# Left operands of the first w_up group: made at the start of the up stage, or in the dense stage and kept in DRAM

## The chip, the cores and the metric

The kernel runs on one core of one Trainium2 chip. The metric is the device time of one execution in microseconds, so lower is better. The core has TensorE (PE) for matmuls, VectorE (DVE), ScalarE (ACT), GpSimd (POOL) and SyncE (SP). DMAs are issued from the queues of SP, ACT and POOL.

## The reference

One layer of an encoder on 2048 tokens of width 1024, all in fp32:

```python
h = rms_norm(x, norm_mix[l])
z = h @ w_in[l]                      # 1024 -> q, k, v of two attentions and two gates
...
merged = (gates[..., :D_MODEL] * (y_a @ w_proj_a[l])
          + gates[..., D_MODEL:] * (y_b @ w_proj_b[l]))
x = x + merged @ w_out[l]
h2 = rms_norm(x, norm_mlp[l])
x = x + jnp.square(jax.nn.relu(h2 @ w_up[l])) @ w_down[l]    # 1024 -> 4096 -> 1024
return rms_norm(x, norm_final)
```

y_a is attention within a window of 128 tokens, y_b attention within a neighbourhood of a token grid.

## The kernel before

Every fp32 operand of a matmul is split into a rounded part (hi, a cast on ScalarE, L277) and the rest (lo, a subtraction, L278), and a product is the sum of three fp32r matmuls, hi·hi, hi·lo and lo·hi (L281, L282, L283). The large products are done by blocks of 2 x 2 with Strassen's seven products, so both operands are also sums and differences of blocks; a product is named by its number n from 1 to 7.

The stages follow each other in time: the dense stage (w_in, up to about 540 us), the two attentions and gates (to about 1170), the out stage (w_out, two halves m of the tokens, to about 1370), the up stage (w_up, to about 1993) and the down stage (w_down).

*Dense stage.* Quads q = 2 to 13 of columns of w_in are computed one after the other (`in_seeded`); each quad has seven products, and beside each product one step of a generator `prep` is issued. Such generators prepare later stages: `wo_parts` makes the left operands of the out stage from w_out and keeps them in DRAM (wo_d), `h1_sums` makes sums of right pages (h1sum). Their small tiles zc (ring `in_c`) and xin are shared with the stage's own work. The tiles of v (quads 6 and 12) are turned by TensorE (L392, from zc into PSUM), cast by ScalarE (L405), subtracted by VectorE (L406) into ze and written by SP to vs_b (L456).

*Up stage.* Its left operands are parts of w_up: for each group q of 512 columns `up_left_steps` makes seven operands [128, 2, 4, 256] (hi and lo, 1 MB) from two raw tiles uraw, in rings uwhla (one buffer) and uwhlb (two). Its right operands are pages ubh of h2, read back from DRAM (h2d) into uraw and urb, scaled (L548 on ScalarE, L551 on VectorE) or cast and subtracted. The order of the products is 1, 5, 6, 2, 7, 4, 3. An output block is emptied from PSUM (tile b) into uc. The first group's work is issued within the out stage's second half, m = 1, by `up_start`: `up_weights` loads two raw tiles (L1265), products 1 and 5 have their lo parts on VectorE, and the steps from product 6 on use GpSimd (`eng=G`): its rows are L272 (differences) and L278 (lo parts).

The program is written in issue order, and a scheduler that goes by the modelled times of the whole program sets the order on each engine's queue. So a change in one place shifts instructions near it and near those that depend on it. Within a queue the order is kept: what stands behind a waiting instruction waits too. A name such as zv stands for a tile that may belong to a ring of one or more buffers; a new user of a buffer waits until the last reader has finished.

Of the kernel before, what the change touches and what calls it, by code (L numbers as in the profile page):

```python
# [8 lines left out]
F32 = mybir.dt.float32  # L9
F32R = mybir.dt.float32r  # L10
AF = mybir.ActivationFunctionType
ALU = mybir.AluOpType
# [10 lines left out]
P = 128  # L23
KC = D // P
NB = 4
BT = 512
# [66 lines left out]
def encoder_layer(ctx, tc, x, norm_mix, w_in, b_gate, sink, rpb, w_pa, w_pb, w_out,  # L93
                  norm_mlp, w_up, w_down, norm_final, dist_a, mask_b, out):
    nc = tc.nc
    V, A, G, PE, SY = nc.vector, nc.scalar, nc.gpsimd, nc.tensor, nc.sync
# [16 lines left out]
    dp = pool("dp", space=DRAM)  # L113
# [157 lines left out]
    def add(eng, out, a, b, op=ALU.add):  # L271
        return eng.tensor_tensor(out=out, in0=a, in1=b, op=op).ins  # L272
# [400 lines left out]
    def wo_parts(k, own):  # L673
# [24 lines left out]
        for n, src in ((2, b21), (5, t1), (7, t3), (6, b12), (4, b11)):  # L698
            part(n, src)
            yield  # L700

    def own():
        return T(xp, [P, D], F32, "xin", 3)

# [52 lines left out]
    for q in range(2, len(QUADS)):  # L757
        if q != SECOND + 1:
            prep = iter(())
        steps, b0 = 1, 0  # L760
        if q == 5:
            prep = wo_parts(0, own)
        elif q in (6, 7):
            k = 2 * (q - 6)
            prep, steps = in_turn((h1_sums(k), h1_sums(k + 1))), 2
        elif q == SECOND - 1:
            prep = h1_right(right2)
        elif q == len(QUADS) - 1:
            prep = h1_last(right2)
        elif q >= SECOND and q != SECOND + 1:  # L770
            n_wo[0] += 1
            prep = wo_parts(n_wo[0], own)
        if q == SECOND:
            right, b0 = right2, 2
        elif q > SECOND:
            b0 = 2
        next(prep, None)
        if q == 11:
            bias_tables()
        lf = list(in_left(ws, QUADS[q][1], (1, 2) if q == 2 else (), ORDER if q == 2 else ORDER_3))  # L780
# [475 lines left out]
    def up_whl():  # L1256
        n_whl[0] += 1
        return (up_rings["whla"] if n_whl[0] % 3 == 1 else up_rings["whlb"])()

    def up_weights(q, behind=None):  # L1260
        ws = []
        for p in range(2):
            w = up_rings["raw"]()
            with tc.issue_after(behind) if behind else nullcontext():
                SY.dma_start(w, w_up[0][p * BT : (p + 1) * BT, q * BT : (q + 1) * BT].rearrange("(k p) f -> p k f", p=P))  # L1265
            ws.append(w)
        return ws
# [5 lines left out]
            pass  # L1273
        return out

    def up_left_steps(ws, out, behind=None, eng=V):

        a11, a21 = ws[0][:, :, 0:256], ws[0][:, :, 256:512]
        a12, a22 = ws[1][:, :, 0:256], ws[1][:, :, 256:512]

        def parts(src, eng):
            hl = up_whl()
            split(src, hl[:, 0], hl[:, 1], eng)
            return hl
# [9 lines left out]
        add(eng, a21, a11, a21, ALU.subtract)  # L1294
        s2 = up_rings["S"]()
        add(eng, s2, a22, a21, ALU.subtract)
        out[6] = parts(s2, eng)
        yield
        out[2] = parts(a12, eng)
        yield  # L1300
        out[7] = parts(a21, eng)
        yield
        out[4] = parts(a22, eng)
        last_left[0] = rounded[0]
        yield
        add(eng, a12, a12, s2, ALU.subtract)
        out[3] = parts(a12, eng)
# [201 lines left out]
    def up_start():  # L1509

        up_homes("raw", "whla", "whlb", "bh1", "bh5", "S")
        rights, lf = up_right(0), {}
        next(rights)
        yield
        next(rights)
        ws = up_weights(0, wo_dma[0])
        yield
        rest = up_left_steps(ws, lf, eng=G)
        started.extend((rights, lf, rest))
        for _ in range(2):  # L1520
            next(rest)
        yield
# [169 lines left out]
    for m in range(2):  # L1692
# [4 lines left out]
        ws = None  # L1697
# [200 lines left out]
```

## Time and profile before

| What | Value |
|---|---|
| Times of three runs | 2610.56, 2615.22, 2616.41 us; median 2615.22 |
| Profiled execution | 2613.9 us, span 2612.1 us, mean granted clock 0.996 |
| Busy in the span: PE, DVE, ACT, POOL | 97%, 65%, 50%, 16% |
| DMA | 552.39 MB, mean 211 GB/s |

In the rows of the profile, a time at the left is the start in the span, the next number the duration; a group's row gives its count behind an x, then the busy time and the mean of one. In square brackets stands how long the engine had been idle and what released it. A row of waits gives the total, how often, and the longest. A window's row gives for PE, PEld (weight load), DVE, ACT and POOL the busy microseconds and the number of instructions, then the granted clock of TensorE, the share of DMA time that was busy, and GB/s. DMA rows give the issue's line and queue (SPq, ACTq, POOLq), the size, and the time from issue to landing.

### The profile page before, as it was taken

Reading aid. Unit: us, or ns where it says so; the run is one execution under the profiler, and the core shown is the slowest. Engines: PE = TensorE matmul, PEld = TensorE weight load, DVE = VectorE, ACT = ScalarE, POOL = GpSimd, SP = SyncE. Lnnn points to the kernel's source line nnn. Section 1 sums busy time; section 2 is a strip of 40 time slices with the busy share of each in tenths; the row PEclk is TensorE's granted clock in tenths of the full one; section 3 lists DMA queues with packets and bytes.
Section 4 is the critical chain, followed back from the end, with each engine's and each line's share of the span. In section 5 each row is a group of like instructions: output and inputs, shape, how many; then the busy total and the mean of one; then the engine's idle time right before and its main releaser. Section 6 shows DMA issues by size and latency. Waiting matters only on the chain.

```text
span 2612.1 us, 34574 instructions
## 1 busy us (share of the span) xinstructions
PE 2546.5 (97%) x11936; PEld 2116.3 (81%) x11936; DVE 1702.0 (65%) x2693; ACT 1310.8 (50%) x2345; POOL 412.2 (16%) x506
## 2 busy tenths in 40 slices
PE   7999999999999998999998999999999999999998
PEld 6788888877877987888887888888887888888887
DVE  8867577667675575745589667766665535554766
ACT  6365464557765674614356555644444322323444
POOL 1000101133345764221312000000000000000011
PEclk9999999999999999999999999999999999999999
DMA  5768868774348998788887665854428825445554
GB/s 186 217 197 247 282 226 275 234 219 114 93 137 208 223 273 233 228 283 315 271 330 246 234 226 201 290 169 152 155 103 303 299 97 185 145 151 164 185 197 166
DMA packets 347695, 552.39 MB, mean 211 GB/s; under 512 B 32072, under 2 KB 152376, under 8 KB 345472
## 3 DMA queue, kind: packets, MB, share of 16 engines
q1 hardware_dynamic: 330336, 509.66, 61.0%
q10 hardware_dynamic: 10944, 24.12, 2.5%
q0 software_dynamic: 6240, 16.40, 2.1%
q8 instruction: 94, 1.54, 0.2%
q14 instruction: 81, 0.66, 0.1%
HBM read 363.35 MB, written 186.71 MB: 211 GB/s over the span
## 4 chain that ended last, share of the span: by engine, by line
PE 76%; DMA 11%; DVE 7%; ACT 3%; issue 2%; SPq 1%; POOL 1%; DVEq 0%; POOLq 0%; ACTq 0%
PE b L282 15%; PE b L283 15%; PE b L281 15%; PE zb L281 5%; PE zb L283 5%; PE zb L282 5%; PE mm L202 2%; PE mm L204 2%; PE mm L203 2%; DMA vb<-vs_b 2%; PE av L1117 1%; DMA z<-zg 1%; PE pt L1137 1%; PE pt L887 1%; DMA uraw<-h2d 1%
## 5 line engine op out<-in xcount | busy, mean ns | idle before, releaser
L282 PE MATMUL b<-dwh,dah 128*128 128x512 f32 x896 | 348.7, 389 | 0.4 <-DVE dwh L278 0.4
L283 PE MATMUL b<-dwh,dah 128*128 128x512 f32 x896 | 347.7, 389 | 0.0
L281 PE MATMUL b<-dwh,dah 128*128 128x512 f32 x896 | 338.3, 389 | 1.6 <-ACT dwh L277 1.6
L277 ACT CAST dah<-da 128x1024 fp32r<-128x1024 f32 (+1 forms) x128 | 120.9, 945 | 368.6 <-PE b L283 245.8
L281 PE MATMUL zb<-zh,zwhl 128*128 128x512 f32 x728 | 284.3, 391 | 4.8 <-DVE zc L272 2.0
L282 PE MATMUL zb<-zh,zwhl 128*128 128x512 f32 x728 | 284.7, 391 | 0.0
L283 PE MATMUL zb<-zh,zwhl 128*128 128x512 f32 x728 | 283.4, 391 | 1.2 <-DVE zwhl L278 1.1
L278 DVE TENSOR_TENSOR dah<-da,dah 128x1024 fp32r<-128x1024 f32 (+1 forms) x128 | 139.2, 1089 | 213.9 <-ACT dah L277 212.0
L281 PE MATMUL b<-ubh,uwhlb 128*128 128x512 f32 x592 | 230.2, 389 | 2.6 <-ACT uc L1472 1.6
L282 PE MATMUL b<-ubh,uwhlb 128*128 128x512 f32 x592 | 230.4, 389 | 1.2 <-DVE ubh L278 1.2
L283 PE MATMUL b<-ubh,uwhlb 128*128 128x512 f32 x592 | 229.0, 389 | 0.0
L281 PEld LDWEIGHTS b<-dwh,dah 128*128 128x128 f32 x896 | 168.2, 188 | 36.9 <-ACT dwh L277 2.1
L282 PEld LDWEIGHTS b<-dwh,dah 128*128 128x128 f32 x896 | 168.2, 188 | 35.7 <-DVE dwh L278 0.8
L283 PEld LDWEIGHTS b<-dwh,dah 128*128 128x128 f32 x896 | 168.2, 188 | 34.8
L272 DVE TENSOR_TENSOR uc<-b,uc 128x512 f32<-128x512 f32 x160 | 109.1, 689 | 114.2 <-PE b L283 107.8
L281 PEld LDWEIGHTS zb<-zh,zwhl 128*128 128x128 f32 x728 | 136.7, 188 | 35.3 <-ACT zc L488 2.5
L283 PEld LDWEIGHTS zb<-zh,zwhl 128*128 128x128 f32 x728 | 136.7, 188 | 30.4 <-DVE zwhl L278 2.5
L282 PEld LDWEIGHTS zb<-zh,zwhl 128*128 128x128 f32 x728 | 136.7, 188 | 27.7
L202 PE MATMUL mm<-zh,whl 128*128 128x512 f32 x368 | 155.7, 423 | 0.6 <-ACT z L465 0.6
L204 PE MATMUL mm<-zh,whl 128*128 128x512 f32 x368 | 145.5, 395 | 0.0
L203 PE MATMUL mm<-zh,whl 128*128 128x512 f32 x368 | 145.0, 394 | 0.0
L281 PEld LDWEIGHTS b<-ubh,uwhlb 128*128 128x128 f32 x592 | 111.1, 188 | 26.3 <-ACT uc L1472 2.0
(268 smaller groups left out, 5734.9 us busy)
## 6 DMA issues: line engine op xcount, KB each, us to landing
at<-uc SPq DMA_DIRECT2D x224, 256.0 KB, 2.9
da<-at SPq DMA_DIRECT2D x96, 512.0 KB, 3.5
dw<-in_w_down_dram SPq DMA_DIRECT2D x160, 256.0 KB, 5.0
uraw<-in_w_up_dram SPq DMA_DIRECT2D x32, 1024.0 KB, 5.9
pgl<-wo_d SPq DMA_DIRECT2D x28, 1024.0 KB, 7.2
zraw<-in_w_in_dram SPq DMA_DIRECT2D x24, 1024.0 KB
z<-zg SPq DMA_DIRECT2D x64, 256.0 KB, 4.7
qs_a<-ze SPq DMA_DIRECT2D x32, 256.0 KB, 5.4
```

The source lines that it names most:

```text
L202: PE.matmul(ps, lh, rh, start=first, stop=False)
L203: PE.matmul(ps, lh, rl, start=False, stop=False)
L204: PE.matmul(ps, ll, rh, start=False, stop=last)
L272: return eng.tensor_tensor(out=out, in0=a, in1=b, op=op).ins
L277: rounded[0] = A.copy(hi, src).ins
L278: return eng.tensor_tensor(out=lo, in0=src, in1=hi.bitcast(F32), op=ALU.subtract).ins
L281: PE.matmul(ps, lh, rh, start=first, stop=False, skip_group_check=True)
L282: PE.matmul(ps, lh, rl, start=False, stop=False, skip_group_check=True)
L283: PE.matmul(ps, ll, rh, start=False, stop=last, skip_group_check=True)
L887: last = PE.transpose(pt[:, h * P : (h + 1) * P], s[:, h, c * P : (c + 1) * P], ident).ins
L1117: PE.matmul(po[0][:, i0 * P : (i0 + ni) * P], v[:kp, c, :], src[:kp, o : o + ni * P], start=first[0], stop=(c == 7 and z == 1), skip_group ...
L1137: last = PE.transpose(pt[:kp, at + (i - i0) * P : at + (i - i0 + 1) * P], s[i][:, rr : rr + kp], ident)
```

## The change

A new tile `wu_d` in DRAM holds the seven left operands of the first group of w_up. A new generator `wu_parts(k)` makes one of four quarters of them in each of the dense quads 6, 7, 9 and 12: two loads of 256 KB on SP into the tile zv (one buffer), sums and differences on VectorE, four casts on ScalarE, four subtractions on VectorE, and four writes each from ScalarE's and GpSimd's queues. At the start of the up stage `up_loaded` reads the seven operands from `wu_d` by GpSimd's queue. The raw loads, casts, sums and subtractions of the first group's left operands are gone there, and `up_left_steps` has no GpSimd work any more; for the other groups it stays as it was.

```diff
+    WU = (1, 7, 2, 4, 5, 6, 3)
+    wu_d = dp.tile([len(WU), P, 2, 4, 256], F32, name="wu_d")
+
+    def wu_parts(k):
+
+        t = in_v2()
+        for p in range(2):
+            SY.dma_start(t[:, p * BT : (p + 1) * BT], w_up[0][(4 * p + k) * P : (4 * p + k + 1) * P, 0:BT])
+        yield
+        a11, a21, a12, a22 = (t[:, j * 256 : (j + 1) * 256] for j in range(4))
+        u = [in_c(), in_c()[:, 0:256]]
+        s1, s2 = (u[0][:, j * 256 : (j + 1) * 256] for j in range(2))
+        add(V, s1, a21, a22)
+        add(V, a21, a11, a21, ALU.subtract)
+        yield
+        add(V, s2, a22, a21, ALU.subtract)
+        add(V, u[1], a12, s2, ALU.subtract)
+        for n, src in zip((4, 6, 0, 2), (*u, t[:, 0:BT], t[:, BT : 2 * BT])):
+            yield
+            w = src.ap[-1][1]
+            hi = in_c()[:, 0:w]
+            A.copy(hi.bitcast(F32R), src)
+            V.tensor_tensor(out=src.bitcast(F32R), in0=src, in1=hi, op=ALU.subtract)
+            dst = wu_d[n : n + w // 256].rearrange("n p z k c -> p n z k c")
+            for z, part, queue in ((0, hi, A), (1, src, G)):
+                queue.dma_start(dst[:, :, z, k], part.rearrange("p (n c) -> p n c", c=256))
...
+        prep_up = wu_parts((6, 7, 9, 12).index(q)) if q in (6, 7, 9, 12) else iter(())
         next(prep, None)
+        next(prep_up, None)
...
+            next(prep_up, None)
...
+    def up_loaded(out):
+
+        for n in (1, 5, 6, 2, 7, 4, 3):
+            out[n] = up_whl()
+            G.dma_start(out[n].bitcast(F32), wu_d[WU.index(n)])
+            yield
...
-    def up_left_steps(ws, out, behind=None, eng=V):
+    def up_left_steps(ws, out, behind=None):
...
         next(rights)
-        ws = up_weights(0, wo_dma[0])
-        yield
-        rest = up_left_steps(ws, lf, eng=G)
+        yield
+        rest = up_loaded(lf)
```

The change moves instructions on each engine. First SP in the dense stage, where the v tiles of quad 6 are written (vs_b), before:

```order
L456 DMA vs_b_92<-ze_2268 128x1x512 x2
L710 DMA xin_2461<-h1d_96 128x512
L456 DMA vs_b_93<-ze_2292 128x1x512 x2
L710 DMA xin_2461<-h1d_97 128x512
L710 DMA xin_2625<-h1d_96 128x512
L456 DMA vs_b_94<-ze_2323 128x1x512 x2
L710 DMA xin_2625<-h1d_97 128x512
L456 DMA vs_b_95<-ze_2346 128x1x512 x2
```

The same place after; L709 is the load of w_up rows for quad 7's `wu_parts`, and L737 is what was L710:

```order
L456 DMA vs_b_93<-ze_2307 128x1x512 x2
L737 DMA xin_2491<-h1d_96 128x512
L737 DMA xin_2491<-h1d_97 128x512
L456 DMA vs_b_94<-ze_2343 128x1x512 x2
L709 DMA zv_272_2496<-in_w_up_dram 128x512 x2
L456 DMA vs_b_95<-ze_2366 128x1x512 x2
L737 DMA xin_2669<-h1d_96 128x512
L737 DMA xin_2669<-h1d_97 128x512
```

The new load stands ahead of the writes of five of the eight tiles of v, and it waits for the last write from the same buffer by GpSimd's queue.

Second ScalarE at the start of the up stage, from the scaling of page 2 (L548) on, before. ubh_1611 is the hi part of page 7, ubh_1613 that of page 4, and L1434 copies product 2 out of PSUM:

```order
L548 ACTIVATE ubh_1598_13559<-urb_13557,g_mix 128x512 x4
L277 CAST uwhlb_13578<-uraw_13185 128x1024
L277 CAST uwhlb_13581<-uraw_13187 128x1024
L277 CAST ubh_1611_13653<-uraw_13160 128x1024 x2
L1434 ACTIVATE uc_13771<-b_13673 128x512
L277 CAST uwhla_13585<-uraw_13187 128x1024
L1434 ACTIVATE uc_13787<-b_13688 128x512
L1435 ACTIVATE uc_13771<-uc_13771 128x512
L277 CAST ubh_1613_13663<-urb_13557 128x1024 x2
```

After, where L1471 is what was L1434, ubh_1635 is page 7 and ubh_1637 page 4:

```order
L548 ACTIVATE ubh_1623_13668<-urb_13666,g_mix 128x512 x4
L241 ACTIVATE xr_13123<-xr_13123,st_13627 128x1024
L1471 ACTIVATE uc_13871<-b_13773 128x512
L1471 ACTIVATE uc_13887<-b_13788 128x512
L277 CAST ubh_1635_13753<-uraw_13277 128x1024 x2
L1472 ACTIVATE uc_13871<-uc_13871 128x512
L1472 ACTIVATE uc_13887<-uc_13887 128x512
L1469 ACTIVATE uc_13903<-uc_13903 128x512
L277 CAST ubh_1637_13763<-urb_13666 128x1024 x2
```

The casts of the left operands are gone, and the casts of page 7 have moved behind the two copies of product 2.

Third VectorE there, from the lo parts of page 7 on (ubh_1612 before, ubh_1636 after), with those of page 4 (ubh_1614 and ubh_1638), before:

```order
L278 TENSOR_TENSOR ubh_1612_13654<-uraw_13160,ubh_1611_13653 128x1024 x2
L278 TENSOR_TENSOR ubh_1614_13664<-urb_13557,ubh_1613_13663 128x1024 x2
L272 TENSOR_TENSOR uc_13803<-b_13729,uc_13686 128x512
L272 TENSOR_TENSOR uc_13803<-b_13703,uc_13803 128x512
L272 TENSOR_TENSOR uc_13821<-b_13744,uc_13701 128x512
L272 TENSOR_TENSOR uc_13821<-b_13716,uc_13821 128x512
```

The same rows of VectorE after the change:

```order
L278 TENSOR_TENSOR ubh_1636_13754<-uraw_13277,ubh_1635_13753 128x1024 x2
L272 TENSOR_TENSOR uc_13903<-b_13829,uc_13786 128x512
L272 TENSOR_TENSOR uc_13903<-b_13803,uc_13903 128x512
L272 TENSOR_TENSOR uc_13921<-b_13844,uc_13801 128x512
L272 TENSOR_TENSOR uc_13921<-b_13816,uc_13921 128x512
L278 TENSOR_TENSOR ubh_1638_13764<-urb_13666,ubh_1637_13763 128x1024 x2
```

The lo parts of page 4 have moved behind the four steps that empty product 7 out of PSUM. On GpSimd the seven loads stand among the adds of the out stage (m) and the powers (st) of the normalisation: products 5's and 6's ahead of the last two adds, product 1's behind them, product 2's behind six powers, and those of 7, 4 and 3 behind two more.

More of the change, by code (lines that the diff above doesn't have):

```diff
@@ L1293, in up_left_steps @@
         yield
-        add(eng, a21, a11, a21, ALU.subtract)
+        add(V, a21, a11, a21, ALU.subtract)
         s2 = up_rings["S"]()
-        add(eng, s2, a22, a21, ALU.subtract)
-        out[6] = parts(s2, eng)
+        add(V, s2, a22, a21, ALU.subtract)
+        out[6] = parts(s2, V)
         yield
-        out[2] = parts(a12, eng)
+        out[2] = parts(a12, V)
         yield
-        out[7] = parts(a21, eng)
+        out[7] = parts(a21, V)
         yield
-        out[4] = parts(a22, eng)
+        out[4] = parts(a22, V)
         last_left[0] = rounded[0]
         yield
-        add(eng, a12, a12, s2, ALU.subtract)
-        out[3] = parts(a12, eng)
+        add(V, a12, a12, s2, ALU.subtract)
+        out[3] = parts(a12, V)
     h2s_d = {n: dp.tile([BT, BT], F32, name=f"h2sum{n}") for n in (5, 6, 7, 4)}
```

## The prediction

> **What bounds the kernel now.** I read the page first, then the waits of TensorE stage by stage, then the windows and the timeline of the two places that the diff touches: the dense stage, where the new work is put, and the start of the up stage, where the old work is taken away.
>
> ```profile
> PE 2546.5 (97%) x11936; PEld 2116.3 (81%) x11936; DVE 1702.0 (65%) x2693; ACT 1310.8 (50%) x2345; POOL 412.2 (16%) x506
> ...
> 1360.00:1370.00 10.00, 10.00 (x44) 7.99 (x44) 7.96 (x12) 9.59 (x14) 0.00 (x0) 1.00 0.56 219
> 1370.00:1380.00 10.00, 9.32 (x41) 7.37 (x41) 9.32 (x25) 7.45 (x19) 1.66 (x4) 1.00 0.56 190
> 1380.00:1390.00 10.00, 8.96 (x40) 7.13 (x39) 7.30 (x15) 9.11 (x12) 5.88 (x5) 1.00 0.94 233
> 1390.00:1400.00 10.00, 6.79 (x23) 5.01 (x22) 10.00 (x13) 3.34 (x5) 5.11 (x2) 0.83 0.84 200
> 1400.00:1410.00 10.00, 7.82 (x34) 5.97 (x33) 9.10 (x9) 7.03 (x10) 3.72 (x1) 1.00 1.02 357
> ```
>
> TensorE is 97% busy, so only a stretch where it idles can give time back, and any stretch where it is full can only lose. At full speed a window of 10 us holds 44 matmuls (the first row of the windows; 0.227 us each, so 5.4 us for an up product of 24). The four windows after it hold 41, 40, 23 and 34: 38 fewer, about 8.7 us. That is all there is to win at this boundary. What TensorE waits for there:
>
> ```profile
> PE b L282 <- DVE ubh L551: 4.3, 2, 3.2
> PE b L282 <- DVE ubh L278: 1.2, 1, 1.2
> PE b L281 <- DVE uc L272: 1.0, 1, 1.0
> PE b L281 <- DVE xr L272: 0.7, 1, 0.7
> ```
>
> None of these four is a wait for a left operand (uwhla, uwhlb), which is what the change replaces. They are VectorE making the right pages (ubh) and emptying PSUM (xr, uc). So the change can act only through VectorE, ScalarE and the queues, not through the operands themselves.
>
> **What goes, at the start of the up stage.** Two raw loads of w_up, seven casts on ScalarE, three VectorE steps and eight GpSimd steps over 1024 columns. GpSimd's steps slow VectorE when both run:
>
> ```profile
> 1347.23 3.21 DVE L278 TENSOR_TENSOR pgl<-m,pgl 128x1024 fp32r<-128x1024 f32 x1
> ...
> 1359.13 1.20 DVE L278 TENSOR_TENSOR pgl<-m,pgl 128x1024 fp32r<-128x1024 f32 x1
> ...
> 1387.11 2.99 DVE L551 SCALAR_TENSOR_TENSOR ubh<-urb,g_mix,ubh 128x512 fp32r<-128x512 f32 x2 [0.52 <-DMA h2d<-ht]
> ...
> 1390.62 2.30 DVE L551 SCALAR_TENSOR_TENSOR urb<-urb,g_mix,uraw 128x512 f32<-128x512 f32 x1
> 1392.84 2.82 DVE L551 SCALAR_TENSOR_TENSOR ubh<-urb,g_mix,ubh 128x512 fp32r<-128x512 f32 x1
> ...
> 1397.55 0.74 DVE L551 SCALAR_TENSOR_TENSOR urb<-urb,g_mix,uraw 128x512 f32<-128x512 f32 x1
> ...
> 1406.89 2.73 DVE L272 TENSOR_TENSOR uc<-b,uc 128x512 f32<-128x512 f32 x4
> ...
> 1389.92 5.19 POOL L278 TENSOR_TENSOR uwhlb<-uraw,uwhlb 128x1024 fp32r<-128x1024 f32 x2 [1.04 <-ACT uwhlb L277]
> ```
>
> The subtraction pgl takes 1.20 us by itself and 3.21 with GpSimd beside it; the two urb and ubh steps under the 5.19 us of GpSimd took 2.30 and 2.82, and 0.74 once GpSimd was done. TensorE's side of it, product by product:
>
> ```profile
> 1387.83 0.61 PE L281 MATMUL b<-ubh,uwhla 128*128 128x512 f32 x2
> ...
> 1395.71 0.80 PE L282 MATMUL b<-ubh,uwhla 128*128 128x512 f32 x1 [3.21 <-DVE ubh L551]
> ...
> 1399.62 0.62 PE L281 MATMUL b<-ubh,uwhlb 128*128 128x512 f32 x2
> 1401.40 0.50 PE L282 MATMUL b<-ubh,uwhlb 128*128 128x512 f32 x1 [1.16 <-DVE ubh L278]
> ```
>
> Product 2 (left uwhla) runs from 1387.83 to 1399.62, 11.8 us for 5.4. Its two waits on L551 are 3.2 and 1.1 (the 4.3 of the table). Behind the longer one the ten matmuls that were left took from 1395.71 to 1399.62, 3.9 us where ten take 2.3, and the window's granted clock is 0.83: the long idle costs some 1.6 us of slow clock behind it. The last window, with the two waits of 1.0 and 1.2, shows a clock of 1.00.
>
> Worked through with the new order, product by product, in what TensorE loses before and after. *Start:* 0.7 before; the steps that delayed xr are gone: 0. *Product 2:* 4.3 + 1.6 = 5.9 before. Undisturbed, VectorE's five steps of 0.7 us from 1387.1 keep ahead of TensorE; since TensorE now comes 0.7 us earlier and the page does not, I take 0.7. *Product 7:* 1.2 before. In the new order ScalarE's casts of page 7 (ubh from uraw, x2) stand behind the two uc copies that read product 2's PSUM, where before they stood ahead of them:
>
> ```profile
> 1390.71 1.98 ACT L277 CAST ubh<-uraw 128x1024 fp32r<-128x1024 f32 x2
> 1399.35 0.60 ACT L1434 ACTIVATE uc<-b 128x512 f32<-128x512 f32 x1 [6.66 <-PE b L283]
> ```
>
> So after product 2 ends come two copies (0.6 each; L1434 in these rows), a cast (1.0) and VectorE's subtraction (1.2): 3.4 us before the second matmul of product 7 can run, plus up to 1.6 of slow clock: 3.4 to 5.0. *Product 4:* 1.0 before. Its page's subtractions now stand behind the four uc steps of product 7 (2.73 us, of which 1.1 start before the product ends) and need 1.2: about 2.8. *Product 3:* 0 before; its casts move back with the rest: 0 to 1.5, I take 0.8. Sum before 0.7 + 5.9 + 1.2 + 1.0 = 8.8 (the window count says 8.7); after, with 4.1 for product 7, 0 + 0.7 + 4.1 + 2.8 + 0.8 = 8.4. **Boundary: −0.4**, from −4 (no slow clock, page 7 partly ahead) to +3.
>
> The seven replacing loads of 1 MB stand on GpSimd's queue. No 1 MB load of that queue is in this trace; the nearest rows:
>
> ```profile
> uraw<-in_w_up_dram SPq DMA_DIRECT2D x32, 1024.0 KB, 5.9
> pgl<-wo_d SPq DMA_DIRECT2D x28, 1024.0 KB, 7.2
> ...
> wo_d<-zc ACTq DMA_DIRECT2D x28, 256.0 KB, 4.0
> wo_d<-xin POOLq DMA_DIRECT2D x28, 256.0 KB, 5.2
> ...
> uraw<-h2d SPq DMA_DIRECT2D x4, 1024.0 KB, 11.4
> ...
> 1378.89 2.10 POOL L234 TENSOR_TENSOR st<-st,power 128x1 f32<-128x1 f32 x4 [8.10 <-DVE st L232]
> ```
>
> The load that binds is product 2's: in the queue it stands behind two of the four powers at 1378.89, so it goes out near 1380 and is wanted at 1387.1. Between 5.2 us (the queue's own row) and 11.4 it lands at 1385.2 to 1391.4: no cost, or up to 4.3. I take 6.6, between the two SP rows nearest in size, without cost. The Trainium skill ("DMA: Bandwidth & Descriptors", section on the anatomy of one DMA on the GpSimd path) gives 2.0 us + bytes / 436e3 there, 4.4 us for 1 MB, an estimate by which the load would land at 1384.4 and the sum stay the same.
>
> **Out stage.** One wait there, 0.5 us:
>
> ```profile
> PE b L281 <- DMA pgl<-wo_d: 0.5, 1, 0.5
> ```
>
> The two pgl loads now stand ahead of the xr loads and h2d writes on SP, so they go some microseconds earlier: −0.5. Against it, two of the new loads go out among GpSimd's adds near 1292 and share the DMA engines with z<-zp: 0 to +1.5. **Net 0.**
>
> **What is added, in the dense stage.** Four times (quads 6, 7, 9, 12): 2 loads of 256 KB on SP; 8 VectorE steps; 4 casts and 4 DMA issues on ScalarE; 4 DMA issues on GpSimd. Its pattern is that of wo_d's preparation:
>
> ```profile
> L684 ACT CAST zc<-xin x28: 612/622/641, 215.5 to 498.2; 128x512 fp32r<-128x512 f32 x28
> L685 DVE TENSOR_TENSOR xin<-xin,zc x28: 679/684/715, 218.3 to 498.9; 128x512 fp32r<-128x512 f32 x28
> L687 ACTq DMA_DIRECT2D wo_d<-zc x28: 326/328/1251, 216.2 to 498.9; - x28
> DMA to landing us min/median/max: 2.3/5.1/8.1
> ...
> 256.00:310.00 54.00, 53.45 (x251) 44.00 (x251) 34.08 (x42) 29.16 (x40) 7.07 (x13) 1.00 0.85 271
> ```
>
> Three subtractions of 0.68 and five steps of half that width (0.34 to 0.68, I take 0.5) are 4.6 us of VectorE for each quad; three casts of 0.62, one narrower and four issues of 0.33 are 3.7 us of ScalarE. Both are idle for 20 and 25 of the 54 us at 256 to 310, so the total is covered. What is not covered is order: TensorE is full here, and the v transposes (L392) hang on a short chain.
>
> ```profile
> PE zb L392 <- DVE ze L406: 0.6, 1, 0.6
> ...
> ACT ze L405 <- DMA vs_b<-ze: 9.5, 4, 3.7
> ...
> 280.00:285.00 5.00, 5.00 (x25) 4.09 (x24) 3.25 (x4) 1.07 (x2) 0.00 (x0) 1.00 0.95 306
> ...
> 281.91 9.87 SPq L456 DMA_DIRECT2D vs_b<-ze  x10
> ```
>
> TensorE's only wait from 200 to 540 is there, and ScalarE's step L405 already waits 9.5 us for vs_b writes to land, with the DMA engines 95% busy. The new order puts quad 7's load of w_up on SP in the middle of these writes; it reuses a single buffer and so waits until GpSimd's last wu_d write of quad 6 has landed (2.3 to 8.1 us by the landing row of wo_d, after an issue near 275 to 276, so 278 to 284, where SP comes by at 281). Five of the eight tiles' writes are queued behind it. SP thus stands 0 to 3 us, and 1.8 MB more is written into full DMA engines. I put 1 us each on the transposes of quads 6 and 12 and nothing on quads 7 and 9: **+2**, from 0 (the transposes have slack) to +8 (rival B).
>
> **Sum.** −0.4 + 0 + 2 = +1.6 on the profiled execution (span 2612.1, 2613.9 with what lies around it): 2615.5 us. That execution stands 1.3 us below the median of the runs shown (2615.22), inside their spread. A measurement of this kernel tells 0.2%, 5.2 us, from no change: the forecast is no change that can be told.
>
> **Rivals.** *A, the boundary really opens (faster).* If page 7's casts do not wait for product 2's end, or the chain behind it is shorter than summed because each engine has lost its queue of work, 1 to 2 of the 8.8 us remain, and the dense stage hides its work: −7 + 0, 2607. For it: the slow VectorE rows vanish for certain. Against it: the order rows of page 7 and page 4.
>
> *B, the dense stage loses (slower).* The held SP queue delays vs_b's writes, then L405, L406 and L392: at 3 us lost in each of quads 6 and 12 and 1 us in each of the others, 8 us on the −0.4, so 2621.5. It decides when the wu_d write lands over 3 us later than SP arrives, that is near the 8.1 end of its row. For it: the one wait that TensorE has there, and the 95%.
>
> *C, the loads on GpSimd's queue come late (slower).* The load of product 2 lands at 1391.4 and takes 4 us from the same place, while its 1 MB delays the h2d writes that page 2 waits for: +4 on the sum, 2619.5. The Trainium skill ("SBUF — State Buffer", section on two separate sides) warns that a DMA of GpSimd's queue stands still while VectorE runs in a two-port mode. The rows for it here are only the 1.2 us between wo_d's two queues.
>
> **Chances.** Forecast 0.38, A 0.20, B 0.26, C 0.12, 0.04 for the rest. Of the forecast 0.33 lies within 0.2% and 0.05 above it. Of A 0.17 is faster, 0.03 the same; of B 0.21 slower, 0.05 the same; of C 0.06 each; of the rest 0.02 faster and 0.02 slower. Faster 0.19, same 0.47, slower 0.34. The range goes from A's 2607 to 2624, just past B's 2621.5.
>
> **What would show it.** Right: no GpSimd step beside VectorE from 1340 to 1405, product 2's wait for L551 under 1 us, product 7's wait for ubh at L278 near 3 us with uc copies of ScalarE just ahead of the casts, and a little over 2 us of TensorE waits at L392 around quads 6 and 12. Wrong: matmul counts of 43 or more in all windows from 1370 to 1410 (A); waits of over 3 us on L392 or on a quad's left operands between 260 and 515 (B); a wait of TensorE on a DMA of uwhla from wu_d (C).

## The result and the profile after

The changed kernel takes 2627.58 us (median of 7 runs, 2620.23 to 2636.30) against 2615.22 us (7 runs, 2608.78 to 2618.37): a ratio of 1.0054, 95% interval 1.0039 to 1.0069. It is slower by about 12 us in the medians; no change that can be told was forecast. The profiled execution of after took 2636.3 us (span 2634.1) and is the slowest of its kernel's runs, so its 22 us against before's profile are more than the change costs on average.

Where the 22 us come in, by the lag of the same matmul behind its time in before: 8.2 us at the end of the dense stage, 13.3 at the end of the attentions, 19.3 after the out stage, 21.8 in the up stage. The mean granted clock is 0.991 (before 0.996), about 13 us of the span.

The dense stage. TensorE's waits up to 540 us in after (total, times, longest); only the rows that are new or have grown:

```profile
PE zb L392 <- DVE ze L406: 2.7, 3, 1.4
...
PE zb L281 <- ACT zb L528: 1.8, 1, 1.8
```

The wait on L392 was 0.6 in before, the other was not there. Three windows of this stage, after (PE, PEld, DVE, ACT, POOL with counts; then granted clock, DMA share, GB/s):

```profile
256.00:310.00 54.00, 52.67 (x248) 43.07 (x247) 36.90 (x50) 29.53 (x43) 10.58 (x18) 1.00 0.90 297
...
400.00:460.00 60.00, 58.17 (x254) 47.65 (x253) 44.72 (x56) 30.34 (x45) 11.15 (x16) 0.97 0.85 290
460.00:515.00 55.00, 53.63 (x253) 44.12 (x252) 37.70 (x46) 30.05 (x46) 6.56 (x11) 1.00 0.78 251
```

The second and third of them in before:

```profile
400.00:460.00 60.00, 60.00 (x270) 49.68 (x269) 44.23 (x54) 30.91 (x45) 10.53 (x16) 1.00 0.82 275
460.00:515.00 55.00, 55.00 (x260) 45.47 (x259) 34.24 (x40) 29.45 (x43) 5.19 (x8) 1.00 0.78 237
```

TensorE was full and is not any more: 16 matmuls fewer between 400 and 460, 7 fewer between 460 and 515. VectorE gained 2.8 us in the first window, 0.5 and 3.5 in the others, and still has 15 us and more of room: its total is not the bound.

The lag grows by 1.0 us from 256 to 310 (quad 6), by nothing from there to 400, by 3.8 from 400 to 460, by 1.5 to 515 (quad 12) and by 2.3 at the stage's end, where TensorE waits 3.0 us for the load qa<-qs_a, 1.8 in before. What stands behind the wait for L528, which ends at 406.04, is on ScalarE's queue:

```profile
399.36 0.63 ACT L426 ACTIVATE ze<-zc 128x512 fp32r<-128x512 f32 x1 [5.13 <-DMA qs_a<-ze]
...
402.08 0.63 ACT L426 ACTIVATE ze<-zc 128x512 fp32r<-128x512 f32 x1 [1.59 <-DMA qs_a<-ze]
404.07 0.60 ACT L426 ACTIVATE ze<-zb 128x512 fp32r<-128x512 f32 x1 [1.35 <-DMA qs_a<-ze]
...
405.42 0.57 ACT L528 COPY zb<-zb 128x512 f32<-128x512 f32 x1 [0.25 <-DVE ze L427]
```

Each step L426 fills a buffer ze and waits until the write to qs_a that read it has landed. The copy L528 that TensorE needs stands behind these steps. This is just after quad 9's writes to wu_d (380 to 389 us); from 380 to 400 the DMA share is 0.98, where before had 0.90. Up to 545 us L426 waits 12.1 us for qs_a in all, 7.4 in before.

The out stage. TensorE's waits from 1175 to 1375 in after; in before only pgl<-wo_d stood here (1175 to 1355), 1.5 us:

```profile
PE b L281 <- ACT pgl L277: 3.9, 1, 3.9
PE b L281 <- DMA pgl<-wo_d: 0.8, 1, 0.8
```

What made that cast late, in the timeline of GpSimd in after:

```profile
1306.00 1.25 POOL L1310 DMA_DIRECT2D uwhlb<-wu_d  x2 [3.68 <-PE b L204]
1310.80 2.40 POOL L272 TENSOR_TENSOR m<-z,z 128x1024 f32<-128x1024 f32 x1 [3.55 <-DMA z<-zp]
1319.42 2.34 POOL L272 TENSOR_TENSOR m<-z,z 128x1024 f32<-128x1024 f32 x1 [6.22 <-DMA z<-zp]
```

and of SP and ScalarE:

```profile
1307.90 0.79 SPq L1681 DMA_DIRECT2D z<-zp  x2
```

```profile
1321.79 1.04 ACT L277 CAST pgl<-m 128x1024 fp32r<-128x1024 f32 x1 [7.60 <-POOL m L272]
```

The two 1 MB loads go out at 1306.00, z<-zp 1.9 us behind them; its last piece lands at 1319.4, some 11 us after its issue. The DMA engines are full there. After, then the like stretch of before:

```profile
1306.00:1312.00 6.00, 6.00 (x28) 4.99 (x27) 2.11 (x5) 0.00 (x0) 2.44 (x3) 1.00 1.08 405
1312.00:1318.00 6.00, 6.00 (x28) 4.95 (x28) 1.23 (x1) 1.63 (x2) 1.20 (x1) 1.00 1.01 407
1318.00:1324.00 6.00, 2.13 (x8) 1.44 (x7) 2.21 (x2) 2.21 (x4) 2.84 (x2) 0.78 1.05 387
```

```profile
1299.00:1305.00 6.00, 6.00 (x28) 4.97 (x27) 2.60 (x3) 3.00 (x4) 3.49 (x2) 1.00 0.41 128
```

The start of the up stage. TensorE's waits from 1375 to 1445 in after, then ScalarE's timeline around the second of them:

```profile
PE b L281 <- ACT ubh L277: 3.6, 2, 2.0
PE b L282 <- DVE ubh L278: 2.4, 2, 1.9
PE b L281 <- ACT ubh L548: 1.6, 1, 1.6
PE b L282 <- DVE ubh L551: 0.3, 1, 0.3
```

```profile
1413.81 1.08 ACT L1471 ACTIVATE uc<-b 128x512 f32<-128x512 f32 x2 [3.06 <-PE b L283]
1414.78 1.99 ACT L277 CAST ubh<-uraw 128x1024 fp32r<-128x1024 f32 x2
...
1427.09 1.98 ACT L277 CAST ubh<-urb 128x1024 fp32r<-128x1024 f32 x2
```

The wait for L551 fell from 4.3 to 0.3, as forecast, and pages 7 and 4 now wait behind the uc steps, as forecast. Three of the windows:

```profile
1405.00:1415.00 10.00, 7.35 (x30) 5.13 (x28) 6.90 (x12) 4.80 (x8) 0.99 (x2) 1.00 0.97 337
1415.00:1425.00 10.00, 7.26 (x20) 5.45 (x21) 4.33 (x7) 2.82 (x4) 0.06 (x1) 0.66 1.02 286
1425.00:1435.00 10.00, 7.50 (x32) 5.57 (x31) 6.85 (x9) 7.61 (x11) 0.00 (x0) 1.00 1.00 340
```

These three windows hold 82 matmuls, where 30 us at full speed hold 132, and the windows beside them are full. By this count, which is the prediction's own, 11.4 us are lost, where 8.7 were lost before and 8.4 were forecast: 7.9 are waits, about 2.4 the half clock behind page 7's wait (13 matmuls took 5.3 us from 1418.5 on, 2.9 at full speed), the rest small gaps behind each wait.

### The profile page after: what moved, and what is told of

The parts are those of the page before. It is cut to its first block, busy times and chain, and to the rows that moved or that the text cites. A ratio compares the mean times of both kernels' runs of the same rounds, so it can differ in the third digit from the quotient of the medians.

```text
span 2634.1 us, 34701 instructions
## 1 busy us (share of the span) xinstructions
PE 2556.3 (97%) x11936; PEld 2122.9 (81%) x11936; DVE 1702.1 (65%) x2722; ACT 1310.0 (50%) x2354; POOL 404.0 (15%) x521
## 4 chain that ended last, share of the span: by engine, by line
PE 69%; DMA 10%; DVE 4%; issue 4%; ACT 2%; SPq 1%; POOL 1%; DVEq 0%; POOLq 0%; ACTq 0%
PE b L282 16%; PE b L283 16%; PE b L281 16%; PE mm L202 2%; PE mm L203 2%; PE mm L204 2%; PE av L1147 2%; DMA vb<-vs_b 2%; PE zb L281 1%; PE zb L283 1%; PE zb L282 1%; PE pt L1167 1%; PE pt L917 1%; PE s L1121 1%; DMA uraw<-h2d 1%
## 5 line engine op out<-in xcount | busy, mean ns | idle before, releaser
L277 ACT CAST dah<-da 128x1024 fp32r<-128x1024 f32 (+1 forms) x128 | 120.9, 945 | 367.8 <-PE b L283 244.1
L278 DVE TENSOR_TENSOR dah<-da,dah 128x1024 fp32r<-128x1024 f32 (+1 forms) x128 | 139.1, 1088 | 212.9 <-ACT dah L277 212.5
```

The lines of the kernel that those rows point to most:

```text
L277: rounded[0] = A.copy(hi, src).ins
L278: return eng.tensor_tensor(out=lo, in0=src, in1=hi.bitcast(F32), op=ALU.subtract).ins
```

## The experiments

"Dense only" means that the operands are made as in the change, but the up stage starts as in before and reads none of them. Ratios are against before on the same chip and can differ by a thousandth from the quotient of the two medians. The times in us are medians from several chips, so experiments are compared by their ratios.

**1. Which half loses?** *e1_dense_only*: the up stage's start as in before.

```diff
-        rest = up_loaded(lf)
+        ws = up_weights(0, wo_dma[0])
+        rest = up_left_steps(ws, lf, eng=G)
```

> The dense stage's part of the change alone: the operands are made and written to DRAM, but nobody reads them, and the start of the up stage is that of before. Theory (three places lose: the dense stage some 6 to 8 us, the out stage some 6 because two 1 MB loads on GpSimd's queue stand ahead of the last z<-zp loads, the up start some 3): 5 to 8 us slower than before, ratio 1.002 to 1.003, with waits of TensorE at L392 and L281 (ACT zb) between 260 and 515 and no wait at pgl longer than before's. Rival 1 (the dense stage is the whole loss, later waits only follow from it): 12 us slower. Rival 2 (the dense stage is covered, the loss is all at the loads and pages): no change.

Measured 2620.30 us, 1.0040 (1.0027 to 1.0054): about 10 us, between the theory's 5 to 8 and rival 1's 12. *e2_up_loads_only*: the other half; the operands' loads read wo_d, and nothing is made in the dense stage.

```diff
-            G.dma_start(out[n].bitcast(F32), wu_d[WU.index(n)])
+            G.dma_start(out[n].bitcast(F32).rearrange("p z k c -> p z (k c)"), wo_d[n][0].rearrange("k p z c -> p k (z c)"))
```

> The up stage's part of the change alone: seven loads of 1 MB on GpSimd's queue at the start of the up stage, here from wo_d, which holds operands of the same size (so the up stage's values are not the layer's), and nothing made in the dense stage. Theory (the extra loads fall into a stretch of the out stage where the DMA engines are full, and the pages at the up start come late): 4 to 9 us slower than before, with one wait of 3 to 4 us near 1310 (pgl) and page waits of 9 to 10 us at the up start, each with half clock behind it. Rival (the up stage's part is neutral, the dense stage is the whole loss): within 3 us of before.

Measured 2617.37 us, 1.0012 (1.0000 to 1.0024). That is 3 us, below the 4 to 9 expected and on the edge of the rival. The dense half carries most of the loss, the other half a little; together 1.0052. Its waits in the out stage, where the cast of pgl came late by less than in after:

```profile
PE b L281 <- ACT pgl L277: 1.4, 1, 1.4
PE b L281 <- DMA pgl<-wo_d: 1.3, 1, 1.3
```

**2. Was GpSimd beside VectorE worth removing?** *e4_before_vector* is before with the steps on VectorE.

```diff
-        rest = up_left_steps(ws, lf, eng=G)
+        rest = up_left_steps(ws, lf, eng=V)
```

> The kernel before, with the eight GpSimd steps of the first group's left operands on VectorE. It tells whether GpSimd beside VectorE is what costs TensorE time at the up start. If it is, the slow steps of VectorE (2 to 3 us where 0.7 to 1.2 is usual) go, and although VectorE gets 8 steps of 1.2 us more the kernel loses at most 2 us or gains up to 3. If the pages wait for something else, VectorE's 10 us more make it 3 to 8 us slower.

Measured 2615.81 us, 1.0022 (1.0009 to 1.0035). VectorE's steps are short (L278 at 1.17 each, the first row), yet TensorE waits at the next page instead:

```profile
1356.83 2.34 DVE L278 TENSOR_TENSOR pgl<-m,pgl 128x1024 fp32r<-128x1024 f32 x2
```

```profile
PE b L282 <- DVE ubh L278: 3.6, 1, 3.6
PE b L281 <- DVE uc L272: 2.0, 2, 1.3
```

So the slow rows were there, but the boundary is not opened by moving GpSimd's steps to VectorE. VectorE has those eight steps more here; that it does not open without them either is seen in the changed kernel above.

**3. The loads in the out stage.** *e3_loads_late*: the whole change, loads queued behind GpSimd's last sum m.

```diff
+            with tc.issue_after(last_add[0]):
                 G.dma_start(out[n].bitcast(F32), wu_d[WU.index(n)])
```

> The changed kernel with the seven loads queued behind GpSimd's last add of the out stage, so that they no longer run beside the last z<-zp loads. Theory of three places: the wait of about 4 us at the out stage and the slow clock behind it (3.4 us more) go, 5 to 7 us faster than the changed kernel, so still 5 to 8 slower than before. Rival (the z<-zp loads were late for another reason, or the wait comes back as a late load at the up start): within 2 us of the changed kernel.

Measured 2629.80 us, 1.0082 (1.0056 to 1.0107): a miss, no gain. z<-zp is in time, but now three loads go out at 1307.8 to 1309.5 in front of the pgl loads, and these wait:

```profile
PE b L281 <- DMA pgl<-wo_d: 4.7, 2, 3.9
```

```profile
1318.00:1324.00 6.00, 3.53 (x16) 2.60 (x14) 6.00 (x8) 1.65 (x4) 0.00 (x0) 0.98 1.03 374
1324.00:1330.00 6.00, 4.54 (x11) 3.62 (x12) 5.50 (x5) 0.00 (x0) 0.00 (x0) 0.50 1.02 416
```

Not the place in GpSimd's queue costs, but megabytes in a full stretch ahead of a load that TensorE needs soon. *e5_loads_on_sync* puts them on SP, behind the last pgl loads.

```diff
+            with tc.issue_after(wo_dma[0]):
-            G.dma_start(out[n].bitcast(F32), wu_d[WU.index(n)])
+                SY.dma_start(out[n].bitcast(F32), wu_d[WU.index(n)])
```

> The changed kernel with the seven loads on SP's queue behind the last pgl loads, where the raw loads of w_up stood before. If the 2 to 3 MB beside the last z<-zp and pgl loads are what TensorE waits for near 1310 to 1325, that wait (3.9 us in the two kernels with the loads early, with 3.4 us of slow clock) goes: 5 to 7 us faster than the changed kernel, 5 to 8 slower than before. If the wait has another cause (the moved pgl loads on SP), it stays at 3 to 4 us.

Measured 2618.03 us, 1.0022 (1.0006 to 1.0038). Its waits in the out stage, then at the up stage:

```profile
PE b L281 <- DMA pgl<-wo_d: 0.7, 1, 0.7
```

```profile
PE b L281 <- ACT ubh L277: 4.0, 1, 4.0
PE b L282 <- DVE ubh L278: 2.2, 1, 2.2
```

The out stage's wait is gone; the page waits stay. After's 1.0054 falls to 1.0022 by this edit alone, as expected. What the early loads cost on average stays open between 3 us (e2) and 8 us (this edit).

**4. The page order.** *e6_page_order*: page 7's casts are queued ahead of product 2's copies, page 4's subtractions ahead of product 7's uc steps.

```diff
-                    squared(c11[a], ps)
+                    with tc.issue_after(page_marks[7][0]) if m == q == 0 else nullcontext():
+                        squared(c11[a], ps)
...
-                    plus(c22[a], ps, c1[a])
+                    with tc.issue_after(page_marks[4][1]) if m == q == 0 else nullcontext():
+                        plus(c22[a], ps, c1[a])
```

> The changed kernel with the order of before at two places of the up start: page 7's casts on ScalarE ahead of the copies of product 2, and page 4's subtractions on VectorE ahead of the four steps that empty product 7. If that order costs what the prediction said, product 7's and product 4's waits fall from about 6 us to 1 or 2 and the half clock behind them goes: 4 to 7 us faster than the changed kernel. If the pages come late for other reasons (h2d writes landing late), 0 to 2 us.

Measured 2625.17 us, 1.0052 (1.0032 to 1.0073): no gain against after.

```profile
PE b L281 <- ACT uwhlb L277: 7.0, 1, 7.0
PE b L282 <- DVE ubh L278: 2.6, 1, 2.6
PE b L281 <- ACT ubh L548: 1.3, 1, 1.3
```

The wait moved on to the second group's first left operand, whose cast on ScalarE is now the late one.

**5. What in the dense stage costs?** Six dense-only kernels. *e7_dense_no_writes* makes the parts and never writes them:

```diff
-            for z, part, queue in ((0, hi, A), (1, src, G)):
-                queue.dma_start(dst[:, :, z, k], part.rearrange("p (n c) -> p n c", c=256))
```

> The dense part alone without its 32 writes to DRAM: the loads of w_up, the sums, casts and subtractions stay, nothing is written, and the up start is that of before. If the loss of the dense part (10 us in the run of that part alone) is the writes, which fill the DMA engines and hold the SP queue until they have landed, it is at most 2 us slower than before. If it is the steps on VectorE and ScalarE standing in front of the stage's own, it stays at 6 to 10 us.

Measured 2609.72 us, 0.9985 (0.9972 to 0.9999). All the engine steps and the loads cost nothing; between 400 and 460 TensorE is full:

```profile
400.00:460.00 60.00, 60.00 (x270) 49.70 (x269) 45.26 (x56) 29.86 (x43) 9.98 (x16) 1.00 0.84 285
```

*e8_dense_pool_loads* loads w_up by GpSimd's queue, so that SP is not held by these loads, and *e9_dense_other_quads* keeps away from the v tiles:

```diff
-            SY.dma_start(t[:, p * BT : (p + 1) * BT], w_up[0][(4 * p + k) * P : (4 * p + k + 1) * P, 0:BT])
+            G.dma_start(t[:, p * BT : (p + 1) * BT], w_up[0][(4 * p + k) * P : (4 * p + k + 1) * P, 0:BT])
```

```diff
-        prep_up = wu_parts((6, 7, 9, 12).index(q)) if q in (6, 7, 9, 12) else iter(())
+        prep_up = wu_parts((7, 8, 10, 11).index(q)) if q in (7, 8, 10, 11) else iter(())
```

> The dense part alone, all writes kept, but the loads of w_up for it go by GpSimd's queue, so that SP's queue no longer waits for the wu_d writes to land and vs_b, qs_a and h1d transfers are not held behind them. If that hold is the loss (10 us in the run of the dense part alone, nothing without the writes), 0 to 3 us slower than before. If the volume of the writes in full DMA engines is the loss, it stays at 6 to 11 us, with the vs_b writes landing as late as before (median 7.4 us).

> The dense part alone, all writes kept and SP's loads kept, in quads 7, 8, 10 and 11 in place of 6, 7, 9 and 12, so away from both quads with v transposes. If the loss is a coincidence with the v tiles and their vs_b writes, 0 to 3 us slower than before. If it is the volume, wherever it lands, 6 to 11 us.

Measured 2622.20 us, 1.0029 (1.0017 to 1.0041), and 2621.12 us, 1.0036 (1.0024 to 1.0049). The waits of TensorE from 200 to 545, e8, then e9:

```profile
PE zb L392 <- DVE ze L406: 4.7, 3, 2.7
PE zb L281 <- ACT zb L528: 4.4, 3, 3.3
```

```profile
PE zb L281 <- ACT zb L528: 3.2, 2, 2.7
PE zb L281 <- ACT zwhl L277: 1.2, 1, 1.2
PE zb L392 <- DVE ze L406: 0.5, 1, 0.5
```

Neither the load's hold of SP nor the meeting with the v tiles is the cause. In after the load among quad 6's v tiles (L709 at 283.0) waits for no wu_d write; only the one at 324 does, 3.0 us, away from the v tiles. In e8 these loads are not on SP at all. In e9 the wait on L392 is back at before's size and others have taken its place. The wait for L528 near 405 us has the same steps L426 in front of it in e1 (1.0 us) and e8 (3.3 us). Without the writes (e7) L426 waits 1.6 us in all for qs_a. *e10_sync_other_quads* joins e5 and e9 in the whole change, as e9's diff and e5's.

> The whole change with both repairs: the seven loads on SP's queue behind the last pgl loads, and the dense part in quads 7, 8, 10 and 11. If both losses are where the runs put them, the dense part costs 0 to 3 us and the up start is 2 to 4 better than before: within 3 us of before, at best 4 faster. If the dense loss does not depend on the quads, 5 us slower, as with the loads on SP alone.

Measured 2621.43 us, 1.0033 (1.0019 to 1.0046): the same loss as e9 alone, so with the loads on SP the up stage's side costs nothing that these intervals tell. This is more than either range expected.

**6. Does the loss go with the volume?** Dense only, with less written: *e12_room_only* one write of 256 KB, *e11_half_writes* only the hi parts, *e13_half_by_gpsimd* only the lo parts; and all of it from one queue, *e14_all_by_scalar*. e15_scalar_and_sync is the whole change with e14's and e5's edits. The comment behind a line names the kernel that has it.

```diff
-            for z, part, queue in ((0, hi, A), (1, src, G)):
+            for z, part, queue in ((0, hi, A),):  # e11
+            for z, part, queue in ((1, src, G),):  # e13
+            for z, part, queue in ((0, hi, A), (1, src, A)):  # e14, e15
+            if k == 0 and n == 4:  # e12
```

> The dense part alone with the room in DRAM kept and one write of 256 KB in place of 32: all steps on the engines and all loads stay. If the writes are the loss, no change from before, as without any write and without the room. If what costs is where the other tensors lie in DRAM once 7 MB stand before them, 6 to 10 us slower, as with all writes.

> The dense part alone with only the rounded halves written: 16 writes on ScalarE's queue, 3.6 MB, and none by GpSimd's. If the loss goes with the volume of the writes, about half of what the dense part costs: 3 to 5 us slower than before. If GpSimd's queue or the buffers that its writes hold are the loss, 0 to 2 us; if ScalarE's queue, which waits for semaphores of other DMAs before it issues, is the loss, 7 to 10 us.

> The dense part alone with only the lo halves written: 16 writes on GpSimd's queue, 3.6 MB, none on ScalarE's. It has the volume of the run with the rounded halves alone (3 us slower than before, where all 32 writes cost 10). If volume is the cause, 2 to 4 us slower again. If GpSimd's queue is (its writes wait behind wo_d's and h1sum's, and these behind them), 6 to 9 us.

> The dense part alone with all 32 writes on ScalarE's queue. If the volume is the cause, 8 to 11 us slower than before, as with the writes on two queues. If GpSimd's queue is, 3 to 5 us: the first 16 writes cost 3, and 16 more issues of 0.33 to 0.4 us on ScalarE add little.

> The whole change with GpSimd's queue out of it: the writes on ScalarE's queue, the loads of the up stage on SP's behind the last pgl loads. If GpSimd's queue is the cause in the dense stage, 0 to 3 us slower than before, since the loads on SP alone came to 5.7 slower. If it is the volume, 5 to 8 us slower.

| Written in the dense stage | Kernel | us | Ratio, 95% |
|---|---|---|---|
| nothing | e7 | 2609.72 | 0.9985 (0.9972 to 0.9999) |
| 256 KB | e12 | 2614.78 | 1.0005 (0.9993 to 1.0016) |
| 3.7 MB by ScalarE's queue | e11 | 2615.82 | 1.0011 (0.9999 to 1.0023) |
| 3.7 MB by GpSimd's queue | e13 | 2617.00 | 1.0010 (0.9997 to 1.0022) |
| 7.3 MB by ScalarE's queue | e14 | 2620.68 | 1.0026 (1.0011 to 1.0040) |
| 7.3 MB by both, three placements | e1, e8, e9 | 2620.30 to 2622.20 | 1.0040, 1.0029, 1.0036 |
| whole change, e14's and e5's edits | e15 | 2619.82 | 1.0016 (1.0005 to 1.0028) |

The loss grows with what is written, about −1, 3 and 9 us for next to nothing, half and all (means of the dense-only rows' ratios), and does not depend on the queue beyond the intervals. Whether it is proportional, these intervals can't tell: e14's 6.8 us and e15's 4.2 lie between the two ranges expected of them.

The lag of the same matmul behind before's profiled run, at 580 us, says that the loss arises in the dense stage. It is 1.7 to 12.6 us in the ten profiled runs that write all of wu_d there, −0.4 and 6.7 in the two that write half (e11, e13), and −3.2 to −0.1 in the seven that write 256 KB or nothing there. Later stages can give some of it back (e13 is at 0.5 by 1260 us).

So it is shown that the loss comes with the writes. What of them costs is not separated: the bytes, the number of transfers and the buffers that are held until a write has landed go up and down together in these runs. One such hold can be told apart: ScalarE's casts L723 waited 5.9 us for wu_d writes to free zc in after and 0.6 in e9, which lost as much.

**7. The same work where the DMA engines have room.** Between 620 and 780 us before's DMA share is 0.29 to 0.48. *e17_attention_only* makes the operands there, in eight pieces of half the columns, in tiles of their own; *e16_parts_in_attention* adds the loads as in e5.

```diff
+    def with_parts():
+        gens = [wu_parts(i) for i in range(8)]
+        steps = iter([g for g in gens for _ in range(7)])
+        for u in range(14, 32):
+            if u >= 15:
+                with tc.issue_after(began[-1]):
+                    for g in islice(steps, 4):
+                        next(g, None)
+            yield attn_a(u, *units_a[u])
...
```

> The whole change with two moves: the operands are made beside the windowed attention's second half (about 650 to 800 us, where the DMA engines of the changed kernel are 30 to 48% busy) instead of in the dense stage, in eight pieces of 128 columns in four tiles of their own, and the seven loads go from SP behind the last pgl loads. Theory (what the dense stage loses is the written volume where the DMA engines are 85 to 95% busy): the same 7.2 MB costs nothing here, so of e5's 1.0022 and e15's 1.0016 the dense stage's 3 to 4 thousandths go: 0.998 to 0.999, about 5 us below before. Rival (the volume is not it; VectorE and ScalarE work of about 35 us each has to be paid wherever TensorE waits for them, and they are 70% busy here): 1.002 or more, with waits of TensorE on sa, ph and pl between 650 and 800 us longer than before's.

> Only the making of the operands in the attention, as in e16; the up stage starts as in before and reads none of them. Theory (volume in full DMA engines): 1.000, against 1.0026 to 1.0040 for the same work in the dense stage. Rival (engine work is paid wherever it is put): 1.002 or more.

Measured 2641.43 us, 1.0109 (1.0089 to 1.0130), and 2636.75 us, 1.0096 (1.0077 to 1.0115): far on the rival's side. But these runs did not test the volume. VectorE's waits from 620 to 780 in e17, then TensorE's from 640 to 860:

```profile
DVE wus L273 <- DMA wut<-in_w_up_dram: 13.2, 7, 3.2
```

```profile
PE av L903 <- ACT ph L922: 7.1, 6, 2.4
PE av L904 <- DVE pl L923: 5.7, 9, 2.1
```

The first sum of a piece stood at the head of VectorE's queue until its load had landed, and the attention's steps behind it (ph and pl waits 12.8 us, 2.2 in before). *e18_attention_paced* takes that wait away in e16.

```diff
+                with tc.issue_after(began[-1]), tc.issue_after(ph_pl[-2]), tc.issue_after(ph_pl[-1]):
+                    for _ in range((1, 4, 3)[u % 3]):
+                        next(steps.pop(0), None)
```

> e16 with its waits taken away: in e17's trace VectorE's first sum of seven of the eight pieces stood 13.2 us in all at the head of its queue for its own load, and the attention's steps queued behind it. Here the load goes out one unit of the attention ahead of the sums, the parts follow a unit later, all 32 kinds of write go from ScalarE's queue one step behind, and every step is pinned behind a cast and a subtraction of the attention. Theory (in a stretch with free DMA engines neither volume nor work costs): 0.998 to 0.999, VectorE's wait for the load gone, TensorE's waits on ph and pl between 580 and 800 us as before (2.2 us). Rival (the windowed attention's chain pays for any step put between its own, since TensorE waits for VectorE and ScalarE there): still 1.005 or more, with ph and pl waits of over 8 us although no step waits for a load.

Measured 2625.65 us, 1.0051 (1.0034 to 1.0068). Half the loss of e16 is gone, and with it VectorE's waits for these loads. From 580 to 740 TensorE ran 804 matmuls for 821 in before, but at the last piece ScalarE stood for its own writes with two buffers, and the chain fell to half clock. ScalarE's waits from 735 to 795 in e18, and one window:

```profile
ACT wuh L726 <- DMA wu_d<-wuh: 4.6, 2, 2.4
```

```profile
745.00:750.00 5.00, 5.00 (x15) 4.33 (x16) 3.08 (x10) 2.08 (x7) 0.02 (x1) 0.50 0.87 234
```

So both expectations of 0.998 missed, and the rival's 1.005 and its 8 us are just met: TensorE waited 8.1 us for ph and pl from 580 to 820. It stays open whether the writes would be free there, since in these runs the steps put between the attention's own already cost time.

## Why the prediction was wrong

**The dense stage, "+2, from 0 to +8": mis-sized.** It measured about +9 on the mean (dense-only runs of all writes, 1.0026 to 1.0040) and +8.2 in the profiled run. That VectorE and ScalarE have room was right (e7 costs nothing). So was the price of the transposes: "1 us each" measured 1.3 (0.6 of it in before) and 1.4 of waits in the profiled run. The step that failed is "nothing on quads 7 and 9", a term put at nothing without a row, while 1.8 MB for each quad went into DMA engines that are 0.78 to 0.98 busy. The prediction looked for harm only where the v transposes hang. The profiled run lost 3.8 us between 400 and 460, where ScalarE stood for the landing of qs_a's writes with L528 behind it and half clock followed, and 2.3 at the stage's end. Other quads pay as much (e9), by whichever short chain is next: L392, L528 or zwhl. The landing row taken from wo_d, 2.3 to 8.1 us, was short as well: wu_d's writes of 256 KB from ScalarE's queue have a median of 10.2.

That the writes are the cause is shown (e7, e11 to e14). That qs_a's writes landed late because of them is argued, from the DMA share and from e7; before itself has 7.4 us of this wait without one of TensorE.

**Rival B had the sign and the size, not the place or the mechanism.** It put 8 us on the hold of SP in quads 6 and 12. At quad 6's v tiles SP was not held, and with the load off SP (e8) or off the v tiles (e9) the loss stayed. The lag grew by 1.0 us in quad 6 and by 1.5 around quad 12.

**Out stage, "Net 0": mis-sized.** "0 to +1.5" for two loads among GpSimd's adds measured +6 in the profiled run (lag 13.3 to 19.3): 4.7 us of waits for 1.5, and slow clock behind the longer one. The prediction took this term from no row; before has a DMA share of 0.41 there, a stretch with room. The loads filled it to over 1.0, and 2 MB ahead of a small load that TensorE wants is some 5 us at 400 GB/s, an estimate from these windows. e5 shows it: behind the pgl loads the wait is gone. The "one wait" of 0.5 us that it read is that of the stage's second half; the whole stage has 1.5.

**The boundary, "−0.4": right in its parts, small in its sum.** The wait for L551 was 0.3 (forecast 0.7 for product 2, which waited 1.9 with the 1.6 for L548), page 7's wait 1.6 for L277 and 1.9 for L278 plus about 2.4 of slow clock (forecast 3.4 to 5.0 in all), page 4's 2.0 and 0.5 (2.8), product 3's nothing (0.8). The sum is 11.4 for 8.4, so +2.7 against before, inside its range of −4 to +3. Page 7's waits came out as forecast (3.5 for 3.4). The excess is mostly the clock behind them (2.4 where 0.7 was taken) and page 2's wait (1.9 for 0.7). That page 2's reads of h2d came later because they shared full DMA engines (0.97) with the 1 MB loads is argued, not shown. In e6 the order of before brought no gain: the next late cast stood right behind.

**Rival A, the boundary opens: no.** The slow VectorE rows did vanish, as it said, but page 7's casts waited for product 2's copies all the same.

**Rival C, the loads late: half right.** TensorE never waited for uwhla or uwhlb. The four loads into uwhlb landed later than taken (6.6), and the three into uwhla after a median of 8.0:

```profile
uwhlb<-wu_d POOLq DMA_DIRECT2D x4, 1024.0 KB, 8.6
```

In e5 and e10 the same loads on SP's queue have medians of 7.3 and 7.2 (uwhlb), 9.0 and 9.5 (uwhla), so the queue makes no clear difference. By the Trainium skill ("DMA: Bandwidth & Descriptors", anatomy of one DMA on the GpSimd path) the estimate was 4.4 us; the trace does not agree where the DMA engines are full.

**What is not explained.** Between 650 and 1260 us, where nothing was changed, the profiled run of after lost 5.1 us more; in the profiled runs of e1, e3, e5, e7, e9 and e10 that stretch moved by −2.7 to +2.5. In that of e13 it moved by −6.1. I take it for scatter of a single execution, but no run shows its cause.

## What to carry to other kernels

An engine with free time is not the only thing to look at when work is moved to it: look at what the DMA engines carry in that stretch. Here 7 MB written while they were 78 to 98% busy cost about 9 us, although the engine work with it cost nothing; the loss showed up in whatever short chain hung on the next landing, and moving the writes to another queue or place in the stage did not save it. Put large loads that are wanted later behind the small ones that are wanted next, on the same queue. Ask of every quad or stage that gets new transfers which step waits for a landing there; a place without a wait today is not a place without a price. When TensorE's waits are removed, name the late instruction next in line first: here a cast of a page, a uc copy and a left operand stood one behind the other.

## What the runs showed of the hardware

A wait of TensorE of about 2 us or more is often, not always, followed by a granted clock of one half, seen as 1318 to 1324 (0.78) and 1415 to 1425 (0.66) above; one of 1.8 us at 540 in before was not. In the record of the clock after has eight such stretches of 3.4 or 6.8 us besides the one at its end, 40.8 us together; before has four of 3.4 us, 13.6 together. At half speed that is up to 13.6 us of TensorE's work more, as much as the mean clock of 0.991 for 0.996 says. So where TensorE is busy through such a stretch, a wait costs its length and up to 1.7 or 3.4 us behind it, half of the stretch.

Ahead of page 7's slow stretch, which begins at 1416.9, TensorE waited 1.65 and 1.87 us, two matmuls apart. The Trainium skill ("TensorE: Matmul & The Clock Gate", Part 1) has the clock fall after one idle window of about 3.4 us or more. The stretches' lengths of 3.4 and 6.8 us agree with a window of that size, but no single idle there was that long.

A VectorE subtraction of 1.20 us that took 3.21 us beside GpSimd's steps was back at 1.2 with them moved to VectorE (e4: 2.34 for two), yet that kernel did not become faster.
